# The first four tiles of a gated embedding end one by one, and the next SwiGLU spreads its norm factor in the middle of its third pair

## The chip, the cores and the metric

The kernel runs on one core of a Trainium2 chip. The metric is device time in microseconds (us) of one execution. Engines are called as in the profile: PE (matmuls) with PEld (its weight loads), DVE (VectorE), ACT (ScalarE), POOL (GpSimd) and SP (the queue that issues the weight DMAs).

## What is computed

Two layers of a decoder over 256 tokens of width 1024. Each layer is a half-weighted SwiGLU, a mixer, a second half-weighted SwiGLU and a gated embedding. Every part reads the residual stream `h` through an RMS norm.

```python
for i in range(DEPTH):                       # DEPTH = 2
    h = h + 0.5 * swiglu(rms_norm(h, ffn_a_norm[i]), ffn_a_w1[i], ffn_a_w3[i], ffn_a_w2[i])
    h = h + mixer(rms_norm(h, mix_norm[i]))  # i = 0: MLA and GLA, i = 1: RG-LRU and S5
    h = h + 0.5 * swiglu(rms_norm(h, ffn_b_norm[i]), ffn_b_w1[i], ffn_b_w3[i], ffn_b_w2[i])
    h = h + (p[i] @ ple_w_up[i]) * sigmoid(rms_norm(h, ple_norm[i]) @ ple_w_gate[i])
return rms_norm(h, final_norm)

def swiglu(x, w1, w3, w2):
    return (silu(x @ w1) * (x @ w3)) @ w2
```

All is float32. The change touches one seam only: the gated embedding of layer 0 (`ple0`) and the SwiGLU that follows it (`ffn_a1`).

## The kernel before

`h` lies transposed in SBUF: 8 tiles of 128 channels by 256 tokens. Every matmul is made of three (`mm3`, lines 279 to 281): operands are split into a high and a low fp32r part, and high by high, high by low and low by high are added in one PSUM bank. A weight tile of 128 by 1024 comes in by one 512 KB DMA (line 255), ACT makes its high part `wh` (line 259) and DVE its low part `wl` (line 260). The split tiles have five buffers (`wp`); the raw ones have five as well. The first four tiles of `ple0` have split buffers of their own (`plep`).

A norm is not applied ahead of the projection. `feed` (lines 322 and 323) writes the two parts of `h` times the gain, the projection starts at once, and the factor 1/rms, a row over the 256 tokens called `R`, multiplies the projection's result when it leaves PSUM. For that, `stat` squares each tile of `h` (line 330) and sums (line 337); `summed` adds over the partitions by four matmuls (line 370); `root` takes the inverse root by three Newton steps on a 128 by 2 tile, on POOL or DVE as told (lines 342 to 355); `spread` splits the result on ACT and DVE (lines 304 and 305), spreads it over all partitions by four matmuls (line 387), and ACT copies it out of PSUM as `R` (line 389).

`first4` begins a stage. It runs the first four output tiles side by side, each in a PSUM bank of its own: for each of the eight input tiles k, one `mm3` for each output tile, 96 matmuls in all. At k = `kn` it calls `end_norm` (`summed` and a root on POOL), at the end or at k = `kb` it calls `spread`. `EARLY` (4, 8) and `LATE` (5, 8) are the two pairs of numbers; `LATE` is for a SwiGLU that follows a gated embedding, which is `ffn_a1` alone.

In `ple0` each of the eight output tiles has an `epilogue`: DVE multiplies by `R` (line 493), ACT takes the sigmoid (line 494), DVE multiplies by `up` (line 495) and adds to `h` (line 497), and `h_done` feeds the next stage and adds to the next norm's sum, on POOL for tiles 0 to 4 and on DVE from tile 5 on. In `ffn` the first four tiles are pair 0 and pair 1 (a pair is the two projections of one tile of the hidden layer); the other 20 pairs run one after the other, each pair in one PSUM bank, and the side work of the next mixer (`s5_prep`) is laid between them. PSUM has five banks for such results (`psum`) and three for helpers (`aux`).

Outside the stages with an order written by hand (the first SwiGLU's start and the mixers, `manual_schedule`) a planner lays down each engine's order when the kernel is built; among instructions that it takes to be ready, those earlier in the program go first. On the chip every engine keeps that order and waits where an operand is late. So line numbers in the program tell what goes first where two steps compete, and the trace tells what the order became.

Of the kernel before, what the change touches and what calls it, by code (L numbers as in the profile page):

```python
# [18 lines left out]
P = 128  # L19
D = 1024  # L20
S = 256
KD = D // P
# [55 lines left out]
LAG = 3  # L78
PLE_DVE = 5
FIN0 = "vector"  # L80
LATE = 5, 8
EARLY = 4, 8


# [124 lines left out]
class Kernel:  # L209
# [77 lines left out]
    def first4(self, x, kn, kb, pool=None):  # L287

        ws = [self.weights(pool=pool) for _ in range(4)]
        pts = [self.psum()[:, :S] for _ in range(4)]  # L290
        for k in range(KD):
            if k == kn:
                Rt = self.end_norm()
            if k == kb:
                R = self.spread(Rt)
            for j in range(4):
                self.mm3(pts[j], ws[j], k * P, P, x[0][:, k, :], x[1][:, k, :], k == 0, k == KD - 1)
        if kb == KD:
            R = self.spread(Rt)
        self.Rt = Rt  # L300
        return pts, R

    def split(self, hi, lo, src):
# [95 lines left out]
    def ffn(self, nxt, buf, side=iter(()), late=False):  # L399
        nc = self.nc  # L400
        x = self.nx
        with ExitStack() as ctx:
            gp = ctx.enter_context(self.tc.tile_pool(name=self.name("ffn"), bufs=1))
            self.gap(gp, G_GAP[nxt])
            gh, gl = (self.t(gp, [P, NF, S], n, F32R) for n in ("gh", "gl"))

            def epilogue(f, src):
                ab = self.t(gp, [P, 2, S], "ab", bufs=3)
                s = self.t(gp, [P, S], "s", bufs=3)
                if len(src) == 1:  # L410
                    nc.vector.tensor_mul(ab, src[0].rearrange("p (t s) -> p t s", t=2), R[:, None, :].to_broadcast([P, 2, S]))  # L411
                else:
                    for t in range(2):
                        nc.vector.tensor_mul(ab[:, t, :], src[t], R)
                nc.scalar.activation(s, ab[:, 0, :], AF.Silu)
                nc.vector.tensor_mul(s, s, ab[:, 1, :])  # L416
                self.split(gh[:, f, :], gl[:, f, :], s)

            if self.w0 is None:
                pts, R = self.first4(x, *(LATE if late else EARLY))  # L420
                epilogue(0, pts[:2])
                epilogue(1, pts[2:])
                first = 2
            else:

                pts = []
                for n in range(2 * LAG):
                    f, t = divmod(n, 2)
                    if t == 0:
                        pts.append(self.psum())  # L430
                    w = self.w0 if n == 0 else self.weights(parts=2 if n == 1 else 1)
                    if n == START + 1:
                        Rt = self.root(pt, nc.vector)
                    self.proj(pts[f][:, t * S : (t + 1) * S], w, 0, x, KD)
                    for m in STATS.get(n, ()):
                        self.stat(m, nc.vector)
                    if n == START:
                        pt = self.summed()
                R = self.spread(Rt)
                self.w0 = None  # L440
                self.order.__exit__(None, None, None)
                for f in range(LAG):
                    epilogue(f, [pts[f]])
                first = LAG
            for f in range(first, NF):
                pt = self.psum()
                for t in range(2):
                    self.proj(pt[:, t * S : (t + 1) * S], self.weights(), 0, x, KD)
                    if f < F_SIDE:
                        self.beside(side)  # L450
                epilogue(f, [pt])
            self.begin_norm(nxt, buf)
            for m in range(KD):
                pt = self.psum()[:, :S]
                for a, b in W2_PARTS:
                    w = self.weights()
                    for f in range(a, b):
                        self.mm3(pt, w, (f - a) * P, P, gh[:, f, :], gl[:, f, :], f == 0, f == NF - 1)
                    if m >= M_SIDE:
                        self.beside(side)  # L460
                hm = self.h[:, m, :]
                nc.vector.scalar_tensor_tensor(out=hm, in0=pt, scalar=0.5, in1=hm, op0=ALU.mult, op1=ALU.add)
                self.h_done(m)
# [23 lines left out]
    def ple(self, nxt, buf):  # L487
        nc = self.nc
        up, x = self.up, self.nx

        def epilogue(m, src):
            z = self.t(self.tp, [P, S], "z", bufs=3)
            nc.vector.tensor_mul(z, src, R)
            nc.scalar.activation(z, z, AF.Sigmoid)
            nc.vector.tensor_mul(z, z, up[:, m, :])
            hm = self.h[:, m, :]
            nc.vector.tensor_add(hm, hm, z)
            self.h_done(m, nc.vector if m >= PLE_DVE else nc.gpsimd)

        pts, R = self.first4(x, *EARLY, pool=self.plep)  # L500
        self.begin_norm(nxt, buf)
        for j in range(4):
            epilogue(j, pts[j])
        for m in range(4, KD):
            pt = self.psum()[:, :S]
            self.proj(pt, self.weights(), 0, x, KD)
            epilogue(m, pt)
# [894 lines left out]
```

## Time and profile before

| | us |
|---|---|
| median of three timed runs | 1023.68 (1023.31 to 1025.05) |
| the profiled execution | 1031.07 |
| its span, first to last instruction | 1029.3 |
| PE busy in the span | 1009.5 (98%) |
| DVE busy | 753.1 (73%) |
| ACT busy | 571.4 (56%) |
| POOL busy | 47.1 (5%) |
| DMA | 183.07 MB, mean 178 GB/s |

A busy PE is a modelled time: each matmul of 256 columns has a record of 0.28 us, and the next one starts some 0.11 us after it started, so records overlap. How fast PE goes is read from the number of matmuls in a stretch, not from its busy share. The `x` numbers of a stretch count the records that touch it, so up to two or three too many for the ends.

### The profile page before, as it was taken

To read this page: it belongs to the slowest core of one execution; us is meant where nothing else is said; L and a number is where in the kernel's file an instruction comes from. 1 tells how busy PE (TensorE), PEld (TensorE's weight loads), DVE (VectorE), ACT (ScalarE), POOL (GpSimd) and SP (SyncE) were. 2 spreads that over 40 slices of the span, in tenths; PEclk is the share of its full clock that TensorE was granted. 3 is DMA by queue.
4 is the path that set the end of the run, shared out by engine and by line. 5 is a ranking of instruction groups with operands and counts; after the bars stand their busy time and mean duration, and the time that the engine had idled before them with its cause. 6 is when DMAs were issued, how large, how long until landed. Compare 5 with 4: busy or idle time off the path is not lost.

```text
span 1029.3 us, 21008 instructions
## 1 busy us (share of the span) xinstructions
PE 1009.5 (98%) x8526; PEld 994.3 (97%) x8526; DVE 753.1 (73%) x1350; ACT 571.4 (56%) x926; POOL 47.1 (5%) x134
## 2 busy tenths in 40 slices
PE   9999999999999999999999999999999999999996
PEld 8999999988899999999989999999898999999996
DVE  6877756589677777757689987876878777776665
ACT  7545445456565554546555764644678564545453
POOL 0000000200001000000240000002200000000000
PEclk9999999999999999999999999999899999999998
DMA  7655556465245655566446555564224565555641
GB/s 275 223 201 188 187 193 193 159 201 179 74 147 182 225 191 198 178 200 221 150 144 218 190 197 195 175 196 156 89 83 144 184 207 203 187 190 183 199 165 42
DMA packets 52945, 183.07 MB, mean 178 GB/s; under 512 B 5856, under 2 KB 6768, under 8 KB 52848
## 3 DMA queue, kind: packets, MB, share of 16 engines
q1 hardware_dynamic: 52160, 181.12, 52.7%
q8 instruction: 67, 1.10, 0.4%
q10 hardware_dynamic: 688, 0.61, 0.3%
q14 instruction: 30, 0.25, 0.1%
HBM read 180.13 MB, written 1.05 MB: 176 GB/s over the span
## 4 chain that ended last, share of the span: by engine, by line
PE 88%; DVE 6%; ACT 4%; issue 1%; DMA 1%; POOL 0%; SPq 0%; DVEq 0%; ACTq 0%; POOLq 0%
PE mm L279 26%; PE mm L281 26%; PE mm L280 26%; DVE wl L260 2%; ACT wh L259 1%; DMA h<-in_xT_dram 1%; PE mm L524 1%; PE mm L523 1%; PE mm L522 1%; PE mm L737 1%; PE mm L739 1%; PE mm L738 1%; PE aux L1141 0%; PE aux L1157 0%; PE aux L807 0%
## 5 line engine op out<-in xcount | busy, mean ns | idle before, releaser
L260 DVE TENSOR_TENSOR wl<-raw,wh 128x1024 fp32r<-128x1024 f32 (+2 forms) x350 | 414.8, 1190 | 152.0 <-ACT wh L259 151.4
L259 ACT CAST wh<-raw 128x1024 fp32r<-128x1024 f32 (+2 forms) x350 | 354.5, 1021 | 229.3 <-PE mm L280 108.0
L279 PE MATMUL mm<-xhA,wh 128*128 128x256 f32 x1200 | 331.8, 276 | 0.9 <-ACT xhA L322 0.9
L280 PE MATMUL mm<-xlA,wh 128*128 128x256 f32 x1200 | 332.0, 277 | 0.4
L281 PE MATMUL mm<-xhA,wl 128*128 128x256 f32 x1200 | 331.5, 276 | 0.0
L279 PEld LDWEIGHTS mm<-xhA,wh 128*128 128x128 f32 x1200 | 225.3, 188 | 1.6 <-ACT xhA L322 1.6
L280 PEld LDWEIGHTS mm<-xlA,wh 128*128 128x128 f32 x1200 | 225.3, 188 | 1.0 <-DVE xlA L323 1.0
L281 PEld LDWEIGHTS mm<-xhA,wl 128*128 128x128 f32 x1200 | 225.2, 188 | 0.2 <-DVE wl L260 0.2
L281 PE MATMUL mm<-gh,wl 128*128 128x256 f32 x704 | 195.2, 277 | 0.0
L279 PE MATMUL mm<-gh,wh 128*128 128x256 f32 x704 | 195.2, 277 | 0.0
L280 PE MATMUL mm<-gl,wh 128*128 128x256 f32 x704 | 195.2, 277 | 0.0
L281 PE MATMUL mm<-xhB,wl 128*128 128x256 f32 x576 | 162.1, 282 | 1.4 <-DVE wl L260 1.4
L279 PE MATMUL mm<-xhB,wh 128*128 128x256 f32 x576 | 162.6, 283 | 0.0
L280 PE MATMUL mm<-xlB,wh 128*128 128x256 f32 x576 | 162.2, 282 | 0.1
L281 PEld LDWEIGHTS mm<-gh,wl 128*128 128x128 f32 x704 | 132.9, 189 | 0.0
L280 PEld LDWEIGHTS mm<-gl,wh 128*128 128x128 f32 x704 | 132.1, 188 | 0.0
L279 PEld LDWEIGHTS mm<-gh,wh 128*128 128x128 f32 x704 | 132.1, 188 | 0.0
L281 PEld LDWEIGHTS mm<-xhB,wl 128*128 128x128 f32 x576 | 110.5, 192 | 1.7 <-DVE wl L260 1.6
L280 PEld LDWEIGHTS mm<-xlB,wh 128*128 128x128 f32 x576 | 109.4, 190 | 0.3 <-DVE xlB L305 0.3
L279 PEld LDWEIGHTS mm<-xhB,wh 128*128 128x128 f32 x576 | 109.2, 190 | 0.0
L304 ACT CAST gh<-s 128x256 fp32r<-128x256 f32 x88 | 35.4, 406 | 89.7 <-DVE s L416 89.7
L411 DVE TENSOR_TENSOR ab<-mm,R 128x512 f32<-128x512 f32 x82 | 56.4, 688 | 13.8 <-PE mm L281 12.6
(409 smaller groups left out, 1059.7 us busy)
## 6 DMA issues: line engine op xcount, KB each, us to landing
raw<-in_w_dram SPq DMA_DIRECT2D x309, 512.0 KB, 3.8
raw<-in_w_dram SPq DMA_DIRECT2D x36, 384.0 KB, 3.2
raw<-in_w_dram SPq DMA_DIRECT2D x4, 256.0 KB, 4.8
out_dram<-hg SPq DMA_DIRECT2D x4, 256.0 KB, 2.2
h<-in_xT_dram SPq DMA_DIRECT2D x2, 256.0 KB, 5.5
h<-in_xT_dram SPq DMA_DIRECT2D x1, 512.0 KB, 6.6
K<-kr ACTq DMA_DIRECT2D x2, 256.0 KB, 4.8
bd<-in_bd_dram SPq DMA_DIRECT2D x1, 512.0 KB, 4.6
```

Of the source, the lines that this page charges most:

```text
L259: nc.scalar.copy(wh[:, sl], raw[:, sl])
L260: self.last_split = nc.vector.tensor_sub(wl[:, sl], raw[:, sl], wh[:, sl].bitcast(F32))
L279: mm(out, wh, xh, start=start, stop=False)
L280: mm(out, wh, xl, start=False, stop=False)
L281: mm(out, wl, xh, start=False, stop=stop)
L304: self.nc.scalar.copy(hi, src)
L411: nc.vector.tensor_mul(ab, src[0].rearrange("p (t s) -> p t s", t=2), R[:, None, :].to_broadcast([P, 2, S]))
L522: mm(pt, a, wh, start=k == 0, stop=False)
L523: mm(pt, b, wh, start=False, stop=False)
L524: mm(pt, a, wl, start=False, stop=k == KD - 1)
L737: mm(pg[name][i], a, wh, start=k == 0, stop=False)
L738: mm(pg[name][i], b, wh, start=False, stop=False)
```

## The change

In `ple`, `first4` is replaced by a loop of its own. The first half is as before (k = 0 to 3, all four tiles at each k). Then come the four matmuls of `summed`, and the root, now on DVE. The second half goes tile by tile: tile 0 with k = 4 to 7, then tile 1, then `spread`, then tile 2, then tile 3. So tile 0 ends 12 matmuls ahead of the `spread`, tile 1 right ahead of it, and the `spread` itself stands 24 matmuls earlier than it did.

In `ffn` of `ffn_a1`, `first4` is told not to spread. The third pair starts with its first projection (24 matmuls), then comes `spread`, then its second projection, and then the epilogues of the pairs 0, 1 and 2. The statistics of that norm and their root on POOL stay where they were. Other stages that call `first4` keep their order.

```diff
-LATE = 5, 8
+LATE = 5
@@ first4
+        self.Rt = Rt
+        if kb is None:
+            return pts
         if kb == KD:
             R = self.spread(Rt)
-        self.Rt = Rt
         return pts, R
@@ ffn
-                pts, R = self.first4(x, *(LATE if late else EARLY))
+                if late:
+                    pts = self.first4(x, LATE, None)
+                    held = self.psum()
+                    self.proj(held[:, :S], self.weights(), 0, x, KD)
+                    R = self.spread(self.Rt)
+                    self.proj(held[:, S:], self.weights(), 0, x, KD)
+                else:
+                    pts, R = self.first4(x, *EARLY)
                 epilogue(0, pts[:2])
                 epilogue(1, pts[2:])
                 first = 2
+                if late:
+                    epilogue(2, [held])
+                    first = 3
@@ ple
-        pts, R = self.first4(x, *EARLY, pool=self.plep)
+        ws = [self.weights(pool=self.plep) for _ in range(4)]
+        pts = [self.psum()[:, :S] for _ in range(4)]
+        for half in range(2):
+            if half:
+                Rt = self.root(self.summed(), nc.vector)
+            for n in range(16):
+                j, k = (n // 4, 4 + n % 4) if half else (n % 4, n // 4)
+                if half and n == 8:
+                    R = self.spread(Rt)
+                self.mm3(pts[j], ws[j], k * P, P, x[0][:, k, :], x[1][:, k, :], k == 0, k == KD - 1)
```

## Rows read from the trace of the kernel before

**Rows 1.** The page's chain that ended last: share of the span by engine.

```profile
PE 88%; DVE 6%; ACT 4%; issue 1%; DMA 1%; POOL 0%; SPq 0%; DVEq 0%; ACTq 0%; POOLq 0%
```

**Rows 2.** Stretches: us, busy (x instructions) PE, PEld, DVE, ACT, POOL; PEclk, DMA share, GB/s.

```profile
493.00:504.78 11.78, 11.78 (x106) 11.78 (x105) 4.38 (x10) 3.01 (x6) 2.58 (x13) 1.00 0.52 169
515.66:530.78 15.12, 12.87 (x107) 12.30 (x105) 11.65 (x35) 5.70 (x14) 4.52 (x15) 1.00 0.38 132
530.78:717.80 187.02, 187.02 (x1590) 187.02 (x1589) 156.23 (x377) 105.79 (x170) 12.63 (x24) 1.00 0.57 191
```

**Rows 3.** PE's timeline at its two waits: start, duration, work [idle before, releaser].

```profile
518.38 0.28 PE L281 MATMUL mm<-xhB,wl 128*128 128x256 f32 x1
520.06 0.39 PE L281 MATMUL mm<-xhB,wl 128*128 128x256 f32 x1 [1.40 <-DVE wl L260]
...
529.00 0.28 PE L281 MATMUL mm<-xhB,wl 128*128 128x256 f32 x1
530.12 0.39 PE L387 MATMUL aux<-frame,ms 128*128 128x256 f32 x1 [0.85 <-ACT ms L304]
```

**Rows 4.** PE's timeline in `ple0`: the sums, what follows, the spread, what follows.

```profile
498.44 0.62 PE L370 MATMUL aux<-ones,sq 128*128 128x256 f32 x4
498.89 0.28 PE L279 MATMUL mm<-xhA,wh 128*128 128x256 f32 x1
...
504.33 0.28 PE L387 MATMUL aux<-frame,ms 128*128 128x256 f32 x1
```

**Rows 5.** `ple0`, DVE, POOL and ACT timelines: sums read, root's ends, split, `R`, table.

```profile
499.09 0.16 DVE L376 TENSOR_SCALAR ms<-aux 128x2 f32<-128x2 f32 x1 [1.21 <-PE aux L370]
502.78 0.20 POOL L355 TENSOR_TENSOR Rt<-Rt,rt 128x2 f32<-128x2 f32 x1
503.24 0.16 DVE L305 TENSOR_TENSOR rt<-Rt,ms 128x2 fp32r<-128x2 f32 x1 [3.99 <-ACT ms L304]
504.98 0.37 ACT L389 COPY R<-aux 128x256 f32<-128x256 f32 x1 [1.77 <-PE aux L387]
505.37 1.28 ACT L494 ACT_TABLE_LOAD   x1
```

**Rows 6.** The root of `ffn_a0`, on DVE: two of its steps, six instructions apart.

```profile
27.07 0.15 DVE L349 TENSOR_TENSOR rt<-Rt 128x2 f32<-128x2 f32 x1
28.24 0.16 DVE L349 TENSOR_TENSOR rt<-Rt 128x2 f32<-128x2 f32 x1
```

**Rows 7.** DVE's timeline: last tile's product, a late weight split, split of the sum.

```profile
517.39 0.41 DVE L493 TENSOR_TENSOR z<-mm,R 128x256 f32<-128x256 f32 x1
518.79 1.21 DVE L260 TENSOR_TENSOR wl<-raw,wh 128x1024 fp32r<-128x1024 f32 x1
524.88 0.42 DVE L305 TENSOR_TENSOR sq<-acc,sq 128x256 fp32r<-128x256 f32 x1
```

**Rows 8.** `ffn_a1`: POOL's root ends; ACT and DVE until the first product.

```profile
529.65 0.20 POOL L355 TENSOR_TENSOR Rt<-Rt,rt 128x2 f32<-128x2 f32 x1
529.98 2.00 ACT L259 CAST wh<-raw 128x1024 fp32r<-128x1024 f32 x2
531.87 0.36 ACT L389 COPY R<-aux 128x256 f32<-128x256 f32 x1
533.42 1.41 DVE L414 TENSOR_TENSOR ab<-mm,R 128x256 f32<-128x256 f32 x4
```

**Rows 9.** Stretches of steady matmuls: `ffn_b0`, `ffn_a1`, and both sides of `ffn_b1`'s spread.

```profile
326.00:490.00 164.00, 164.00 (x1449) 164.00 (x1449) 116.86 (x154) 86.75 (x126) 0.00 (x0) 1.00 0.62 206
531.00:711.00 180.00, 180.00 (x1531) 180.00 (x1530) 155.91 (x375) 104.40 (x167) 9.83 (x11) 1.00 0.58 195
803.00:823.00 20.00, 20.00 (x172) 20.00 (x171) 14.40 (x28) 10.29 (x19) 1.66 (x9) 1.00 0.57 195
827.00:847.00 20.00, 20.00 (x179) 20.00 (x178) 17.63 (x28) 13.98 (x21) 0.00 (x0) 1.00 0.78 250
```

**Rows 10.** `ffn_b1`'s spread on PE: no idle before it.

```profile
825.88 0.28 PE L387 MATMUL aux<-frame,ms 128*128 128x256 f32 x1
```

## The prediction

> **What bounds the kernel now.** I read the chain that ended last first. PE carries 88% of it [rows 1], so the end moves only where PE waits, or where it runs at a lower rate. Then I read the stretches around the change. Two of them hold the same work. From 493.00 to 504.78 PE does the first four tiles of `ple0`: 96 matmuls, 4 for the sums and 4 for the spread, 104 in 11.78 us, or 113.3 ns each. From 515.66 to 530.78 it does the first four tiles of `ffn_a1`, again 96, 4 and 4, and takes 15.12 us [rows 2]. The difference, 3.34 us, is all that can be won at this seam without doing less work or doing it at another rate. PE's timeline shows where it goes. Between two starts that would be 0.11 us apart there are 1.68 us at 518.38 (DVE's split of a weight tile is late) and 1.12 us at 529.00 (the inverse root is late) [rows 3]. Less one step each these are 1.57 and 1.01 us; the other 0.76 us are slower steps after each restart.
>
> The third thing to read is the rate. In `ffn_b0` 1449 matmuls stand in 164 us, 113.2 ns each; in `ffn_a1` 1531 in 180 us, 117.6 ns each, at the same granted clock of 1.00 (2.4 GHz) [rows 9]. That is a second bound, and I come back to it.
>
> **Part one, `ple0`.** The root goes from POOL to DVE, the spread up by 24 matmuls. DVE has read the sums at 499.25 (499.09 and 0.16). POOL's 13 instructions end at 502.98, 3.73 us later [rows 5]. On DVE the root is ten instructions; the trace has this root on DVE in `ffn_a0`, six steps in 1.17 us, 0.195 us each [rows 6]. Ten make 1.95 us, so it ends at about 501.2. The split and its hand-over took from 502.98 to 503.40, 0.42 us [rows 5], so the spread can start at about 501.65. PE comes to it after 24 matmuls from 498.89, at 501.61 [rows 4]. So PE waits some 0.05 to 0.1 us, or nothing if the planner lays a few matmuls ahead of it; I take 0.1. DVE stood idle for 3.99 us while POOL worked [rows 5], so the ten instructions cost nothing there. Nobody waits for what POOL no longer does.
>
> The spread stood at 504.33 [rows 4] and stands now near 501.7: `R`, whose copy followed by 0.65 us [rows 5], comes 2.6 us earlier. The load of ACT's table right behind it (1.28 us) moves along. Tiles 0 and 1 are finished by then; tiles 2 and 3 end at 503.4 and 504.8, and DVE has no need of them before. So the row of epilogues starts 2.6 us earlier. DVE works from there to the split of the next norm's sum at 524.88 [rows 7], busy 11.65 us of the 15.12 in the first four tiles of `ffn_a1` [rows 2]: it is DVE's queue that made both the weight split and the sum late, since the planner puts epilogues ahead of weight splits. Started 2.6 us earlier, it should end about as much earlier, with one limit: tile 7's product was at 517.39 [rows 7], and its last matmul, one step ahead of 515.66 [rows 2], is done 0.28 us after its start, at 515.83, so this one can move up by no more than 1.5 us.
>
> With 2.6 us the split that PE waited for (518.79 and 1.21, to 520.00) ends at 517.4, ahead of PE's need at 518.5. With 1.5 us it ends at 518.5, just in time. The sum's split, to 525.30, ends at 522.7 or at 523.8; PE, if it waited nowhere, asks for it after 64 matmuls, at 515.66 + 7.25 = 522.9. So what is left of that first wait lies between 0 and 0.9 us. I take 0.3, nearer to the shift of 2.6, since the two queued weight splits (1.21 us each) no longer stand between tile 7's product and the sum once DVE has caught up.
>
> **Part two, `ffn_a1`.** The spread goes down by 24 matmuls, 2.72 us at 113.3 ns. Its operand was 1.01 us late [rows 3]. So that wait is gone, with 1.7 us to spare. All that the spread issues moves: the split on ACT and DVE (0.42 us, off the path as PE still has matmuls to do), 4 matmuls, and the copy of `R`. No DMA moves; SP's loads keep their order. POOL's root stays where it is. What is queued behind the spread on PE is the third pair's second half and then pair 3. The weights for that second half were split on ACT from 529.98 [rows 8], right behind the wait for the root, and will be there about 2 us before PE needs them.
>
> What is late next: `R`. Five banks of PSUM hold the four tiles and the held pair, so pair 3's first matmul needs the bank of the first product. Before, that product ended at 533.83, 3.71 us after the spread's first matmul at 530.12, because ACT had two weight casts (2.00 us) ahead of the copy and DVE two splits ahead of the product [rows 3, 8]. Now pair 3 comes 4 + 24 matmuls after the spread's first, 3.17 us. With the same delays PE waits 0.54 us; but those casts were free to start when the first four tiles had ended, which is now 2.7 us ahead of the spread, so the product should end 1.5 to 2.7 us after it. Between 0 and 0.54 us, I take 0.
>
> **The sum.** 3.34 - 0.1 - 0.3 - 0 = 2.9 us less, by the rate as it is. Against the profiled execution that is 1031.07 - 2.9 = 1028.2 us; against the median of the timed runs, which is 7.39 us below it, 1020.8 us.
>
> **The rate.** The stretch from the end of that spread, 530.78, to 717.80 has 1590 matmuls in 187.02 us [rows 2]. At 113.2 ns they would take 180.0: 7.0 us less. The slow step isn't the clock (1.00 in both) and not the other engines' load: in `ffn_b1` 20 us hold 172 matmuls with DVE busy 14.40 us ahead of the spread, and 179 with DVE busy 17.63 us behind it [rows 9]. Between them lies a spread for which PE did not wait [rows 10]; the slow stretch of `ffn_a1` begins behind one for which it did [rows 3]. So the slow step looks like a state that PE falls into when it restarts after a wait and leaves at an undisturbed spread. If so, the change takes it away from all of `ffn_a1`. But the profile is one execution, and 7.39 us is about what it stands above the timed runs; these may have run `ffn_a1` at the quick step all along. The rows don't tell which.
>
> The Trainium skill, page "TensorE: Matmul & The Clock Gate", section "Back-to-back issue gap", gives the step of isolated matmuls by their columns alone, which for 256 is an estimate of 109.2 ns. The trace does not agree: it has 113.2 and 117.6 ns for the same columns at the same clock. By that rule there would be no second rate to win, and the sum would stay at 2.9 us.
>
> **Rivals.**
> - *A, the forecast*: both waits go, the rate of the timed runs stays as it was: 1020.8 us, 1020.3 to 1022.0. Chance 0.42.
> - *B, the rate too*: the timed runs had the slow step in `ffn_a1` and lose it: 1023.68 - 2.9 - 7.0 = 1013.8 us. For it: all three timed runs agree within 1.8 us, so they share one state, and the one execution that can be seen is in the slow one. Against it: the 7.39 us. Chance 0.33.
> - *C, the wait only moves*: DVE's queue moves up by tile 7's 1.5 us alone, PE waits 0.9 us for the sum, 0.54 us for pair 3's bank, and some 0.8 us of slower steps stay: 1.1 us won, 1022.6 us, not to be told from no change. Also the case that the planner's order undoes what the program's order says. Chance 0.11.
> - *D, slower*: PE stops at pair 3 for the PSUM bank, and restarts at the slow step for the rest of `ffn_a1` where the timed runs had the quick one: 1023.68 - 2.9 + 7.0 = 1027.8 us. It decides from the point at which the first product ends later than 3.17 us after the spread's first matmul (before: 3.71). The same could come of the 0.1 us in `ple0` if the next spread doesn't mend it. Against it: the earlier casts. Chance 0.14. The Trainium skill, page "Trainium Kernel Development and Optimization", section "Best Practices", says that consistent bubbles can mean that SBUF or PSUM ran out; in the trace of before no wait of PE at this seam is for a bank.
>
> **How the numbers follow.** The predicted time is A's, 1020.8 us. The range goes from 1013.0 (B with its bounds) to 1024.0; D and a little of B lie outside. This kernel's measurement tells about 0.2%, 2.05 us, from no change, which is at 1021.6. B is faster (0.33), and of A all but the cases near 1022 (0.36): faster 0.69. C and the rest of A: within 0.2%, 0.17. D: slower, 0.14.
>
> **What would show it.** In the trace after: `ple0`'s spread near 501.7 with next to no idle ahead of it; the first sigmoid some 2.6 us earlier; no idle of PE at DVE's weight splits, and the spread of `ffn_a1` with none; `ffn_a1` from its start to the end of its spread in about 14.5 us (128 steps of 113.3 ns); pair 3 starting without a wait. The count of matmuls in 180 us of `ffn_a1` tells the rate: 1590 would be the quick step, 1531 the slow one. I am wrong if PE's idle turns up at pair 3, if the epilogues of `ple0` don't move by 2 us or more, or if the spread of `ple0` waits for the root.

## The result and the profile after

The changed kernel takes 1029.22 us (median of 9 runs, 1027.25 to 1035.71) and the kernel before, on the same chip, 1024.52 us (9 runs, 1021.66 to 1025.89). The ratio is 1.0058, 95% interval 1.0041 to 1.0074: slower by 0.6%, or 4.7 us, outside the predicted range. The profiled execution took 1030.06 us, span 1028.3 us. The one of before happened to run `ffn_a1` at the slow step [rows 9] and this one at the quick step, so the two spans cannot be set against each other stage by stage.

For that I use the profile of an experiment below, the kernel before with one memset on another engine (`before_cx_on_dve`). It has the waits of before, ran `ffn_a1` at the quick step, and is timed like before. First PE's stretches in it, from `ple0`'s first matmul: to the first matmul of `ffn_a1`, to its sums, to its spread, and on to the first matmul that reads `BT` (line 1158, in the changed kernel 1180), some 20 us into the next mixer. The columns are those of [rows 2], for PE alone.

```profile
494.30:516.97 22.67, 22.67 (x203) 1.00 0.31 104
516.97:526.21 9.24, 7.83 (x66) 1.00 0.47 158
526.21:531.46 5.25, 4.37 (x38) 1.00 0.30 98
531.46:720.80 189.34, 186.81 (x1645) 1.00 0.60 194
```

The same four stretches of the changed kernel:

```profile
494.25:517.10 22.85, 22.85 (x202) 1.00 0.42 141
517.10:524.88 7.78, 7.24 (x62) 1.00 0.43 153
524.88:532.61 7.73, 7.65 (x65) 1.00 0.01 2
532.61:725.84 193.23, 186.81 (x1622) 0.98 0.60 190
```

The change moves 24 matmuls, 2.72 us, from the fourth stretch to the third. With that taken out, `ple0` is 0.18 us longer, the way to the sums 1.46 us shorter, the way to the spread 0.24 us shorter, and all that follows 6.61 us longer (193.23 - 189.34 + 2.72): 5.1 us lost in sum, against 4.7 us by the timed runs. So up to the spread the seam gave 1.5 us of the 3.34, and more was lost behind it. PE's timeline of the changed kernel shows where. The first pair of rows answers to the first of [rows 3], the second is a wait at the sums, the third is new.

```profile
518.23 0.28 PE L280 MATMUL mm<-xlB,wh 128*128 128x256 f32 x1
518.65 0.39 PE L281 MATMUL mm<-xhB,wl 128*128 128x256 f32 x1
...
524.21 0.28 PE L281 MATMUL mm<-xhB,wl 128*128 128x256 f32 x1
524.88 0.97 PE L372 MATMUL aux<-ones,sq 128*128 128x256 f32 x3 [0.40 <-ACT sq L306]
...
535.67 0.28 PE L281 MATMUL mm<-xhB,wl 128*128 128x256 f32 x1
539.45 0.58 PE L279 MATMUL mm<-xhB,wh 128*128 128x256 f32 x1 [3.50 <-DVE ab L416]
```

There is no wait at the spread any more. At 535.67 PE stops for 3.78 us, 3.67 beyond a step, with pair 3's first matmul, which needs the PSUM bank of the first product (`ab`, line 416). The stretches behind it (PE alone) show a second loss:

```profile
535.00:540.00 5.00, 1.50 (x11) 0.82 0.63 179
540.00:545.00 5.00, 5.00 (x26) 0.50 0.73 234
545.00:550.00 5.00, 5.00 (x45) 0.99 0.56 187
```

The granted clock was 0.50, the lower of the two levels (1.2 GHz), for the 5 us that followed the stop: 26 matmuls where 45 stand in the next 5 us.

Why is the product late? DVE's timeline of the changed kernel, from the split of the sum to the products (in [rows 7] the same split stands at 524.88, in [rows 8] the products at 533.42):

```profile
524.86 0.43 DVE L307 TENSOR_TENSOR sq<-acc,sq 128x256 fp32r<-128x256 f32 x1 [0.47 <-ACT sq L306]
530.09 0.16 DVE L307 TENSOR_TENSOR rt<-Rt,ms 128x2 fp32r<-128x2 f32 x1 [3.93 <-ACT ms L306]
531.05 2.36 DVE L260 TENSOR_TENSOR wl<-raw,wh 128x1024 fp32r<-128x1024 f32 x2 [0.80 <-ACT wh L259]
533.33 4.36 DVE L934 TENSOR_SCALAR esr<-cst 128x16 f32<-128x16 f32 x1
533.40 4.29 DVE L260 TENSOR_TENSOR wl<-raw,wh 128x1024 fp32r<-128x1024 f32 x1
537.72 0.17 DVE L935 TENSOR_SCALAR esk<-esr 128x16 f32<-128x16 f32 x1
537.83 1.23 DVE L260 TENSOR_TENSOR wl<-raw,wh 128x1024 fp32r<-128x1024 f32 x1
538.97 1.41 DVE L416 TENSOR_TENSOR ab<-mm,R 128x256 f32<-128x256 f32 x4
```

A group of several instructions (x2, x4) has the time of all of them. The row to look at is 533.33: an instruction on 128 by 16 elements, side work for the next mixer, takes 4.36 us instead of 0.17, and the weight split queued behind it 4.29 instead of 1.2. Both end at 537.69. POOL's timeline of the same stretch:

```profile
529.77 1.82 POOL L1060 MEMSET xhA<- 128x2048 f32 x1
531.52 1.82 POOL L1060 MEMSET xlA<- 128x2048 f32 x1
533.27 4.38 POOL L1060 MEMSET cx<- 128x5120 f32 x1
```

The memset of `cx` begins 0.06 us ahead of `esr` and ends at 537.65. ACT's timeline shows what would have been late without it:

```profile
529.87 0.19 ACT L306 CAST ms<-Rt 128x2 fp32r<-128x2 f32 x1 [5.04 <-POOL Rt L357]
529.96 4.85 ACT L259 CAST wh<-raw 128x1024 fp32r<-128x1024 f32 x5
534.73 0.35 ACT L391 COPY R<-aux 128x256 f32<-128x256 f32 x1
```

Five weight casts stand ahead of `R`'s copy; before there were two [rows 8]. `R` is there at 535.08, and the product starts 3.89 us later.

### The profile page after: what moved, and what is told of

It is laid out like the page before. It is cut to its first block, busy times and chain, and to the rows that moved or that the text cites. A ratio compares the mean times of both kernels' runs of the same rounds, so it can differ in the third digit from the quotient of the medians.

```text
span 1028.3 us, 21022 instructions
## 1 busy us (share of the span) xinstructions
PE 1006.4 (98%) x8526; PEld 990.5 (96%) x8526; DVE 756.3 (74%) x1360; ACT 573.0 (56%) x926; POOL 43.9 (4%) x121
## 4 chain that ended last, share of the span: by engine, by line
PE 82%; DVE 8%; ACT 4%; issue 3%; DMA 2%; POOL 0%; SPq 0%; DVEq 0%; ACTq 0%; POOLq 0%
PE mm L279 24%; PE mm L280 24%; PE mm L281 24%; DVE wl L260 3%; ACT wh L259 2%; DMA raw<-in_w_dram 1%; PE aux L1180 1%; PE mm L547 1%; PE mm L546 1%; PE mm L545 1%; DMA h<-in_xT_dram 1%; PE mm L760 1%; PE mm L762 1%; PE mm L761 1%; PE aux L1164 0%
```

## The experiments

Every ratio is to the kernel before, run beside it on the same chip. Edits are made to the changed kernel where nothing else is said, and `...` stands for lines left out.

Theory P: POOL's memset keeps `esr` off SBUF's port, the split and the products queue behind it, and pair 3 waits for their bank. Rivals: DVE or ACT is late by its own queue (Q), or the loss belongs to part one. The Trainium skill, page "SBUF — State Buffer", section "Who interferes with whom", speaks for P: DVE and GpSimd share one pair of ports as an exclusive lock for a whole instruction; `tensor_scalar` can take the pair (its two-port mode), while an instruction with two SBUF inputs contends only with a GpSimd instruction that reads SBUF.

**`part1_alone`.** `ple0` as changed, `ffn_a1` as before.

```diff
-                if late:
-                    pts = self.first4(x, LATE, None)
...
+                pts, R = self.first4(x, *((LATE, 8) if late else EARLY))
```

> The gated embedding's new order alone, with the SwiGLU's first four tiles as before. Theory (the loss lies in the SwiGLU's part: PE waits at pair 3 for a PSUM bank because DVE's first product is late): no idle of PE at pair 3, PE's wait for the sum of squares some 0.9 us, the wait for the root some 1 us as before; 0.3 to 1.5 us faster than before (ratio 0.9985 to 0.9997). Rival (the earlier epilogues upset DVE's order and cost the time): 3 us or more slower than before.

Measured: 1024.57 us, ratio 1.0006 (0.9977 to 1.0034). Part one alone neither loses nor gains what can be told. There is no pause at pair 3. `esr<-cst`, the instruction that took 4.36 us in the changed kernel, runs at 523.23 in 0.16 us, and the `esr` that the memset holds (`esr<-q`, 2.96 us) stands behind the products, as before.

**`part2_alone`.** `ffn_a1` as changed, `ple0` as before.

```diff
-        for half in range(2):
...
+        pts, R = self.first4(x, *EARLY, pool=self.plep)
```

> The SwiGLU's new order alone, with the gated embedding as before. Theory: the same idle of PE ahead of pair 3, 3 to 4 us, with the granted clock at half behind it, and 4 to 6 us slower than before (ratio 1.004 to 1.006). Rival (only both parts together do it, since the epilogues of the embedding crowd the seam): the wait at pair 3 under 1 us, and no slower than before.

Measured: 1032.70 us, ratio 1.0074 (1.0054 to 1.0094). Here is the loss: PE waits 4.44 us beyond a step at pair 3, `esr` takes 4.36 us, and the clock falls to 0.50 behind the pause, for some 3 us. The profile ran `ffn_a1` at the slow step.

**`memset_in_pieces`.** The memset of `cx` as eight, on POOL still.

```diff
-        for a in (*BB, CX):
+        for a in BB:
             nc.gpsimd.memset(a, 0.0)
+        for i in range(2):
+            for g in range(0, NST, 4):
+                nc.gpsimd.memset(CX[:, i, g : g + 4], 0.0)
```

> The change, with POOL's memset of cx (4.4 us in one instruction) cut into eight of an eighth; nothing else. Theory (DVE's small TENSOR_SCALAR ahead of the first product is shut out for the whole of that memset): that instruction takes under 1 us, the first product starts some 2.5 to 3.5 us earlier, PE's idle ahead of pair 3 falls from 3.8 us to about 1 us and the clock stays at 1.00; 5 us faster than the changed kernel, about level with before (ratio to before 0.998 to 1.001). Rival (the weight casts ahead of R on ACT and the weight splits ahead of the product on DVE make the wait by themselves): the idle stays at 3 us or more, ratio to before 1.004 or more.

Measured: 1028.92 us, ratio 1.0051 (1.0022 to 1.0079): no better. POOL ran the pieces without a gap (531.83, eight in 4.66 us), and DVE got nothing in between:

```profile
531.88 4.65 DVE L934 TENSOR_SCALAR esr<-cst 128x16 f32<-128x16 f32 x1
537.81 1.41 DVE L416 TENSOR_TENSOR ab<-mm,R 128x256 f32<-128x256 f32 x4
```

So P as I had put it, with a release between pieces, fell; P could stand only if POOL keeps the port through a run of memsets. That left P and Q equal here; `cx_on_dve` tells them apart.

The run showed one more thing. Its pause was longer (3.94 us beyond a step), and the clock stayed at 1.00, in its stretches of PE:

```profile
535.00:540.00 5.00, 1.72 (x15) 1.00 0.58 170
540.00:545.00 5.00, 5.00 (x47) 1.00 0.57 188
```

From the spread to the mixer's first projection PE took 170.45 us here (531.16 to 701.61) and 172.77 in the changed kernel (532.61 to 705.38). Less the pauses of 3.94 and 3.67 these are 166.51 and 169.10: the lower clock, with the slow restart, cost 2.6 us.

**`held_in_aux`.** The held pair gets a bank of the helpers' pool, so pair 3 needs no product to end.

```diff
-                    held = self.psum()
+                    held = self.aux()
```

> The change, with the held third pair in one of the three helper banks of PSUM, so that pair 3 finds the fifth bank free and pair 4 is the first to wait for a product. Theory (the bank is what PE waits for): no idle ahead of pair 3, little or none ahead of pair 4 (the first product ends near 539.4, pair 4 starts near 541.2), clock at 1.00, though DVE is shut out as long as before; 5 to 7 us faster than the changed kernel and 0.5 to 2 us faster than before (ratio to before 0.998 to 0.9995). Rival (DVE's late queue shows up wherever PE next needs it): the idle moves to pair 4 or 5, 2 us or more, and the time stays above before by 2 us.

Measured: 1023.53 us, ratio 0.9982 (0.9960 to 1.0004). `esr` still takes 4.38 us and the products still start at 537.86, but PE doesn't stop. The bank is what turns a late product into a pause; with a spare bank the same delay of DVE costs PE nothing at pair 3.

**`cx_on_dve`.** The same zeros, from DVE and later, in ten pieces.

```diff
-        for a in (*BB, CX):
+        for a in BB:
             nc.gpsimd.memset(a, 0.0)
@@ for j in range(L4 + 1): for i in range(2):
+                V.memset(CX[:, i, :, j, :], 0.0)
                 put(CX[:, i, :, j, :], cur[:, i])
```

> The changed kernel, with the zeros of `cx` written by VectorE in ten pieces of 128x512 later on, and no longer by POOL's 128x5120 memset of 4.38 us; the DVE and ACT orders at the seam are the same, wl wl esr wl esk wl ahead of the four products, and five weight casts ahead of R's copy on ACT. Theory (VectorE's esr, 4.36 us in the changed kernel, is held up by that memset): esr takes under 0.3 us, the second pair of weight splits and the products follow ACT's casts, and the first product starts some 3 us earlier, at about 536 by the profile of the changed kernel instead of 538.97. R's copy is still behind five casts (534.73), so pair 3 still waits a little: PE idle 0.3 to 1.2 us there instead of 3.67, and no half clock behind it. Time 1023 to 1026 us. Rival (VectorE's queue itself is late: splits that wait for their casts): esr stays over 3 us or the product stays later than 538, PE idle over 3 us, time about 1029.

Measured: 1022.58 us, ratio 0.9989 (0.9979 to 0.9998). DVE's timeline, same order as in the changed kernel:

```profile
531.86 0.17 DVE L934 TENSOR_SCALAR esr<-cst 128x16 f32<-128x16 f32 x1
531.94 1.22 DVE L260 TENSOR_TENSOR wl<-raw,wh 128x1024 fp32r<-128x1024 f32 x1
533.08 0.17 DVE L935 TENSOR_SCALAR esk<-esr 128x16 f32<-128x16 f32 x1
533.15 1.22 DVE L260 TENSOR_TENSOR wl<-raw,wh 128x1024 fp32r<-128x1024 f32 x1
534.29 1.41 DVE L416 TENSOR_TENSOR ab<-mm,R 128x256 f32<-128x256 f32 x4
```

Pair 3 waits 0.43 us beyond a step. Q falls, but for these 0.43 us: the queues are the same, and the rest of the pause is gone.

**`esr_two_inputs`.** The memset stays on POOL; two instructions of 128 by 16 change their form.

```diff
-        nc.vector.tensor_scalar(out=r, in0=x, scalar1=-87.0, scalar2=88.5, op0=ALU.max, op1=ALU.min)
-        nc.vector.tensor_scalar_mul(k, r, 1.4426950408889634)
+        nc.vector.scalar_tensor_tensor(out=r, in0=x, scalar=-87.0, in1=x, op0=ALU.max, op1=ALU.max)
+        nc.vector.scalar_tensor_tensor(out=k, in0=r, scalar=0.4426950408889634, in1=r, op0=ALU.mult, op1=ALU.add)
```

> The changed kernel with POOL's memset of `cx` (4.38 us) as it is, and two instructions of 128x16 on VectorE in another form: esr and the first esk are scalar_tensor_tensor (two SBUF inputs) instead of tensor_scalar (one). The upper clamp of 88.5 in `exp_small`, which these inputs don't reach, is left out by it. All engine orders are the same. Theory, port by form (VectorE is kept out by a POOL memset only where its own instruction is of a form that takes the shared port as a whole, as tensor_scalar with one fp32 SBUF input, while weight splits with two SBUF inputs went through at 1.22 us beside two other memsets): esr takes 0.2 us beside the memset, the first product comes 3 us earlier, PE's idle at pair 3 is under 1 us, and the time is that of the kernel with `cx` on VectorE, 1022 to 1025 us. The esk behind the products (still a tensor_scalar) may be caught by what is left of the memset, up to 1.5 us, with no bank at stake. Rival (any small VectorE instruction is caught by that memset, or the memset slows whatever VectorE does): esr still takes about 4 us, PE's idle is over 3 us, the time about 1029.

Measured: 1024.71 us, ratio 1.0007 (0.9981 to 1.0032). POOL's timeline, then DVE's:

```profile
531.38 4.40 POOL L1060 MEMSET cx<- 128x5120 f32 x1
```

```profile
531.42 0.17 DVE L934 SCALAR_TENSOR_TENSOR esr<-cst 128x16 f32<-128x16 f32 x1
531.51 1.22 DVE L260 TENSOR_TENSOR wl<-raw,wh 128x1024 fp32r<-128x1024 f32 x1
532.65 0.17 DVE L935 SCALAR_TENSOR_TENSOR esk<-esr 128x16 f32<-128x16 f32 x1
532.73 1.22 DVE L260 TENSOR_TENSOR wl<-raw,wh 128x1024 fp32r<-128x1024 f32 x1
533.87 1.41 DVE L416 TENSOR_TENSOR ab<-mm,R 128x256 f32<-128x256 f32 x4
535.20 0.61 DVE L936 TENSOR_SCALAR esk<-esk 128x16 f32<-128x16 f32 x1
```

Under the full memset `esr` takes 0.17 us, the splits 1.2, and PE waits 0.19 us beyond a step at pair 3 (0.30 us from 534.04 to 534.34). The first instruction that is still a `tensor_scalar`, at 535.20, ends at 535.81, with the memset (531.38 + 4.40 = 535.78). It isn't the memset alone but its meeting with one form of DVE instruction. That is what the page's section says, and here the traces agree.

**`before_cx_on_dve`.** The edit of `cx_on_dve`, made to the kernel before.

> The kernel before, with the zeros of `cx` written by VectorE in pieces. In the trace of before the memset held up esr (2.94 us) just behind the products, where PE had its banks already. Expected: esr under 0.3 us, the seam as before (PE waits of 1.6 and 1.0 us), and the time within 0.2% of before. Rival (the memset's blockade costs the kernel before something too, or VectorE's ten pieces cost more than POOL's one): a difference of over 2 us either way. Its profile also shows once more at which of the two steps `ffn_a1` runs (531:711 with x1531 or with about x1590), in a kernel with before's waits.

Measured: 1024.18 us, ratio 0.9999 (0.9989 to 1.0009). The memset costs the kernel before nothing that can be told, since there the `esr` that it holds stands behind the products.

**`cx_on_dve_held_in_aux`.** Both edits.

> The last kernel, with the bank of the held pair taken from the other pool (aux), so that pair 3 doesn't need the bank of the first product. If the seam's loss is the bank and nothing else, this has no idle at pair 3, as with the held pair in aux alone (1023.5 us), and the memset's place is worth nothing more: 1022.5 to 1024.5 us. If the late products cost something beyond pair 3 (pair 4 and 5 wait for banks in their turn, or the next weights come late), it is faster than 1023.5 by 0.5 us or more.

Measured: 1023.54 us, ratio 0.9988 (0.9973 to 1.0002). From `ple0`'s first matmul to the mixer's first that reads `BT` it takes 225.14 us, and `held_in_aux` 225.16: the two cures don't add, as both only keep pair 3 from waiting.

**`root_on_dve_too`.** The last kernel, and in `first4` the root of `ffn_a1` on DVE.

```diff
-                Rt = self.end_norm()
+                Rt = self.root(self.summed(), self.nc.vector if kb is None else self.nc.gpsimd)
```

> The last kernel, and `ffn_a1`'s root on VectorE too: POOL's 13 instructions of some 3.7 us become ten of 0.2 us on VectorE, so ms is ready 1.8 us earlier and ACT's five casts, which stand behind it, start that much earlier. If ACT's queue behind the root still bounds the seam, PE's remaining waits in the first tiles of `ffn_a1` (0.4 to 0.7 us each at the weight split and at the sums) do not change, since they lie ahead of the root, and there is nothing more to win: within 1 us of the last kernel. If the earlier casts bring later weights forward, 1 us or more less.

Measured: 1022.94 us, ratio 0.9989 (0.9974 to 1.0003); 225.15 us over the same stretch. POOL's root is hidden.

**`sums_on_dve`.** `cx_on_dve_held_in_aux` with `PLE_DVE = 0`: `ple0`'s sums of squares leave POOL.

> The changed kernel with `cx` on VectorE and the held pair in aux, and `ple0`'s four sums of squares on VectorE instead of POOL (PLE_DVE 0). In the changed kernel two of POOL's sums (2.29 us each) run at 513.88 beside VectorE's xlB (1.84 us each, against 0.42 alone). If this contention is what keeps VectorE's end at 1.3 us earlier instead of 2.6: four sums add 4 x 0.42 = 1.7 us to VectorE and take away about 2 x 1.4 us, so the split of the sum comes about 1 us earlier, PE's waits at the sums (0.56 and 0.35 us) shrink to under 0.3 in all, and the time is 0.5 to 1 us under 1023.5. Rival (VectorE's own queue of splits and products is the bound): the sums take the place of what they free, the waits stay, and the time is within 0.5 us of 1023.5 or above it.

Measured: 1021.47 us, ratio 0.9957 (0.9935 to 0.9978), the fastest and clearly faster than before. In the expectation I read 2.29 and 1.84 us as the time of one instruction; they are those of two. Per instruction `xlB` goes from 0.92 to 0.48 us. Its four stretches (PE alone):

```profile
492.78:515.52 22.74, 22.74 (x202) 1.00 0.37 125
515.52:522.83 7.31, 7.08 (x62) 1.00 0.65 188
522.83:530.38 7.55, 7.53 (x66) 1.00 0.08 30
530.38:717.55 187.17, 184.32 (x1622) 1.00 0.61 196
```

The wait for the first of the sums is gone, and 0.18 us is left at the second (0.56 and 0.35 in the changed kernel); the second stretch is 0.45 us shorter. In all the seam is 0.4 us shorter than in `cx_on_dve_held_in_aux`; the ratios to before differ by 0.3%, some 3 us, with intervals that overlap at 0.9973 to 0.9978. A part of that lies in the kernel before: beside this run 8 of its 35 executions took 1030.37 to 1033.01 us, beside `cx_on_dve_held_in_aux` 1 of 35. Against the median of the other 27, 1023.91, `sums_on_dve` wins 2.4 us. Where the rest comes from I did not find.

**`sums_and_root_on_dve`.** The edits of `sums_on_dve` and of `root_on_dve_too`.

> The last kernel, and `ffn_a1`'s root on VectorE too. Expected: the spread has its factor 1.8 us earlier, but PE doesn't wait for it in either, so within 0.5 us of the last kernel; with both, the seam has no POOL work ahead of the spread. This is the candidate for the fastest: 1021.5 to 1023.

Measured: 1022.18 us, ratio 0.9963 (0.9939 to 0.9988): no more than the last.

**`after_again`.** The changed kernel once more.

> The changed kernel once more, beside the others on this chip. If the pause at pair 3 costs 3.67 us always and the half clock behind it comes only in some executions (it came in two of three profiles with such a pause), the executions spread over some 2 us between about 1027 and 1030, and the profile has either about 44 matmuls in the 5 us behind the pause at clock 1.00 or about 26 at 0.50. If the half clock belonged to the pause, every profile would have it.

Measured: 1033.30 us, ratio 1.0058 (1.0031 to 1.0085), the same ratio; the medians alone, 1033.30 and 1024.42, would give 1.0087. The profile has a pause of 3.39 us beyond a step, and the clock stays:

```profile
535.00:540.00 5.00, 2.32 (x19) 1.00 0.62 167
540.00:545.00 5.00, 5.00 (x45) 1.00 0.59 187
```

The half clock came in two of four profiles with such a pause (`part2_alone` and the first of the changed kernel), so it doesn't belong to every pause. The executions spread further than I expected, to 1036.5 us, and this profile ran `ffn_a1` at the slow step (x1502 in 531:711, with the pause inside).

## Why the prediction was wrong

- **The bound of the seam, 3.34 us** [rows 2], held: no run won more. The place of both gains was right. In `cx_on_dve_held_in_aux` the seam gives 1.4 us.
- **Part one, the spread of `ple0`.** Predicted near 501.65 with 0.05 to 0.1 us of wait and 2.6 us earlier for the epilogues. By the profile after, 3.17 us from sums (499.69) to spread (502.86), as predicted, and ACT's table load at 503.99 (505.37 in [rows 5]), while the whole trace lies 1.25 us later at the sums (498.44 in [rows 4]): 2.6 us earlier. The stretch grew by 0.18 us where I took 0.1.
- **What DVE gains from it.** Predicted 1.5 to 2.6 us at the split of the sum; measured against PE's first matmul of `ffn_a1`, 9.22 us before and 7.76 after, 1.46. The residual wait was bounded by 0 and 0.9 and I took 0.3; it was 0.91 at the sums (0.56 and 0.35) and 0.30 more at a weight split. So the term was mis-sized by 0.9 us, by taking the value near the larger shift. Tile 7's product, by which I bounded the shift, did not move up at all: it came 2.48 us after that first matmul (519.58), before 1.73 (517.39). The 1.46 us were won behind it, where DVE has one weight split ahead of the sum instead of three. `sums_on_dve` shows part of why: POOL's sums slow `xlB` beside them, a contention that I had not priced.
- **Part two, the root's wait.** Gone, as predicted, with PE at work up to the spread.
- **Part two, pair 3's bank: the step that failed.** "Between 0 and 0.54 us, I take 0." I listed what was queued on ACT and DVE ahead of the product from the order of before. The order of after has five casts for two on ACT, and on DVE four splits and two side instructions ahead of the products. The casts were free to start when the first four tiles ended, as I said (529.96), but there were five; without the memset's blockade that makes 0.43 us of wait (`cx_on_dve`), inside the bound, at its other end from the value taken. The rest of the 3.67 us is `esr`, the first step of the next mixer's side work, which my list of what moves did not have. Before, this instruction (`esr<-cst`) ran at 524.33 in 0.16 us, ahead of the split of the sum. By the program the steps of the side work are called in the loop over the pairs, which began with pair 2 and now begins with pair 3; in every profile with the new order of `ffn_a1` `esr<-cst` stands between the weight splits ahead of the products. So the change itself put it under the memset. The new order with that call kept at pair 2 was not tried. That the memset can hold such an instruction stood in the trace of before, at the second use of the same helper (`esr<-q`), right behind the products (533.42, [rows 8]), and I didn't read on:

```profile
524.33 0.16 DVE L911 TENSOR_SCALAR esr<-cst 128x16 f32<-128x16 f32 x1
...
534.75 2.94 DVE L911 TENSOR_SCALAR esr<-q 128x16 f32<-128x16 f32 x1
534.82 2.87 DVE L938 TENSOR_TENSOR th<-cst,dt 128x16 f32<-128x16 f32 x1
534.90 2.79 DVE L260 TENSOR_TENSOR wl<-raw,wh 128x1024 fp32r<-128x1024 f32 x1
```

The last three end at 537.69, where POOL's memset of `cx` (533.28 and 4.38) ends. Behind the products such a hold is harmless; ahead of them it is the pause.

- **The sum, remade with the runs:** against the predicted -2.9 us, 0.1 more in `ple0`, 0.9 more at sums and weight split, 3.67 for pair 3's pause, 2.6 for the half clock, and 0.55 for a weight split that is late in the mixer (at 706.51; not there before, but there in every profile with the new order of `ffn_a1` at the quick step, the cures' too). That makes +4.9 us; the stretches gave 5.1, the timed runs 4.7.
- **The rivals.** D was the right place with the right point of decision (3.17 us after the spread; the product came 6.8 us after it), and its time, 1027.8 us, came near by accident: I priced it as a change of rate, and it was a wait and a lower clock. C had the two smaller waits nearly right, 0.9 us at the sum (0.91) and 0.54 at pair 3's bank (0.43 in `cx_on_dve`), and nothing of the side work. B falls: the wait at the spread doesn't set the rate. With before's waits `ffn_a1` ran slow in the profile of before [rows 9] and quick in that of `before_cx_on_dve` (x1581 in 531:711), and the changed kernel ran it quick in one profile and slow in another. In `root_on_dve_too` the profile ran the first SwiGLU, which no edit touches, at the slow step (1276 matmuls in 60:210, 1326 in the others). By these profiles the rate belongs to the execution.
- **Open:** what sets the rate in an execution, why the clock fell in two pauses of four, and why the weight split at 706.51 is late. No run was made for any of these.

## What to carry to other kernels

When a step is moved, list what the engines will run between its old and its new place, side work included, and look for any instruction in the neighbourhood that takes many times its usual time: where it now does no harm it shows the price for the day that one like it stands ahead of something. A long POOL memset is not free because POOL is idle; ask which DVE instructions it will meet, and give the result that holds a scarce PSUM bank a bank to spare. When an order is laid down by a planner, a bound made from the old order bounds the old order only.

## What the runs showed of the hardware

- A POOL memset (4.38 us) held a 128 by 16 `tensor_scalar` on DVE for 4.36 us, and whatever was queued behind it; the same step as `scalar_tensor_tensor` with two SBUF inputs took 0.17 us under the same memset, and weight splits with two SBUF inputs kept 1.2 us. Eight memsets back to back held it for all eight (4.65 us).
- A POOL `tensor_tensor` did slow DVE instructions with two SBUF inputs: `xlB` 0.92 us each beside POOL's sums, 0.48 without.
- After PE stood still for 3.4 to 4.4 us, the granted clock went to 0.50 in two profiles of four and stayed at 1.00 in the others; in the changed kernel it cost 2.6 us.
